# State of the scans: from a running sum in SBUF to identity products in PSUM

## The chip, the cores and the metric

The kernel runs on 1 core of one Trainium2 chip. The metric is device time in microseconds of one execution; three runs of the kernel before gave 2300.24 to 2307.2 us, median 2306.48. Names of engines in the profile: PE is the tensor engine's matmul, PEld its weight load, DVE the vector engine, ACT the scalar engine, POOL GpSimd, SP the queue that issues most transfers.

## The reference, cut to what matters

Two layers are computed for 512 tokens and 256 context tokens of width 1024: an RWKV-7 mixer (layer 0) and a Hyena mixer (layer 1). The change lies in the RWKV-7 scan, which runs once in each direction (z = 0, 1) over context and then over the tokens:

```python
def step(s, inp):
    r_t, w_t, k_t, v_t, a_t, b_t = inp
    sa = jnp.einsum('bhvk,bhk->bhv', s, a_t)
    s = s * w_t[:, :, None, :] + sa[..., None] * b_t[:, :, None, :] + v_t[..., None] * k_t[:, :, None, :]
    return s, jnp.einsum('bhvk,bhk->bhv', s, r_t)
...
for z in range(2):
    yc_z, s_ctx = rwkv7_scan(rc, dc, kdc, vc, kkc, ac, s0, z == 1)
    yx_z, _ = rwkv7_scan(rx, dx, kdx, vx, kkx, ax, s_ctx, z == 1)
```

There are 32 heads of 64 by 64 state; everything is float32.

## The kernel before, in words

The scan is done in chunks of 64 tokens (C): 4 chunks of context and 8 of tokens, so NC = 12 steps of a chain. Heads come in pairs that fill the 128 partitions (p = 0 to 15). One round of the function `chain` takes two pairs (q = 0, 1), two directions (z) and two heads (h) side by side, so a step works on quads of 8 products of 64x64; there are 8 rounds, one after another, 96 steps in all.

A step goes so. The state of head h lies in `sv[h]` on the 64 partitions HR[h]; on the other 64 lie the chunk's values. Eight products of `AR` (keys a, and strictly lower products) with `sv` go to a quad in bank 2 (`bx`, kind pa); ACT copies the half h = 0 to `xs`, DVE the half h = 1. Eight products with the inverse `tt` of a triangular matrix give `bu` (pa again), which ACT and DVE copy, a half each, over the state in `sv`. Then eight products with `BT` (keys b and k, transposed) give `bs` in bank 3 (kind pn, two halves of a bank in turn). DVE adds `bs` to `sc`, a running copy of the state in SBUF, and multiplies it by the chunk's decay `gv`, once for each half, into the next step's `sv`; POOL multiplies `sc` by `gv` as well, in place, for the next step's add. For chunks of tokens (g = 1, 2) eight products `by` of the state with r (ahead of `bu`) and eight more of `sv` with `ARB` (at the step's end) form the output of the step, which the lane `outputs` evacuates.

Round this chain other functions work: `fetch` loads keys, decays and r of a pair and group of four chunks (14 transfers on SP, most of 64 or 128 KB) into rings of GB = 4 and KB = 3 buffers, which the chain gives back when a group of four steps is done; `prep` multiplies them, masks them on DVE and transposes them to `BT` (tile bt, two copies a pair); `merge` loads and completes the inverses; `values` copies values into coming `sv` tiles on ACT or POOL; `readout` and `out_part` turn finished pairs into the layer's output projection (the products whi, wlo with uh, ul). A group's first step begins in program order behind the last copy of its two preparations.

The order on every engine is written ahead of time. Each function is a generator of instructions (a lane); the function `run` picks, by a model of each engine's clock, the instruction that could start first, with a small bias by lane (the chain -0.2 us, preparation 0). Engines then run their own lists in order and wait on semaphores. An instruction made by `copy` with a tuple of engines, or by `either`, is given to the engine on which the model has it done first; the model treats two accesses to one PSUM bank as exclusive. All instructions are emitted in one helper, so that the profile shows line 58 for all of them, and tiles tell them apart: `ps` is any PSUM bank, `cst` the constants (the identity among them).

Of the kernel before, what the change touches and what calls it, by code (L numbers as in the profile page):

```python
# [17 lines left out]
P = 128  # L18
# [7 lines left out]
C = 64  # L26
NCC, NCX = TC // C, TX // C
NC = NCC + NCX
# [211 lines left out]
def net_kernel(ctx: ExitStack, tc: tile.TileContext, I, out, dbg=None):  # L240
    nc = tc.nc
    model = Model()
    V, S, T, G, SP = (Engine(e, n) for e, n in ((nc.vector, "V"), (nc.scalar, "S"), (nc.tensor, "T"), (nc.gpsimd, "G"), (nc.sync, "P")))
    dma = SP.dma_start
    MUL, ADD, SUB = ALU.mult, ALU.add, ALU.subtract
# [81 lines left out]
    def tl(pool, name, shape, bufs=1, dt=F32, tag=None):  # L327
        return model.new(pool, name, shape, bufs, dt, tag)
# [45 lines left out]
    def pt(kind):  # L374
        i = turn[kind]
        turn[kind] = (i + 1) % len(kinds[kind])
        return kinds[kind][i]

    def get(kind):

        return (yield from several(kind, 1))[0]
# [21 lines left out]
    def copy(eng, out, in_):  # L403
        if isinstance(eng, tuple):
            op = copy(eng[0], out, in_)
            op.alts = [op] + [copy(e, out, in_) for e in eng[1:]]
            return op
        if eng is S:
            return S.activation(out=out, in_=in_, func=AF.Copy)
        return eng.tensor_copy(out=out, in_=in_)  # L410
# [14 lines left out]
    def K(name):  # L425
        o, w = CST[name]
        return cst[:, o:o + w]

    ident, ones, cent, ones64 = K("ident"), K("ones"), K("cent"), K("ones64")
# [300 lines left out]
    HR = [slice(0, 64), slice(64, 128)]  # L730
# [261 lines left out]
    n = 2 * sum(g != 3 for g, _, _ in seq)  # L992
# [306 lines left out]
    def rt(name, shape, bufs=1, dt=F32):  # L1299
        return tl(rx, name, shape, bufs, dt)  # L1300
# [14 lines left out]
    xs = rt("xs", [P, 2, 2, 2, C])  # L1315
# [13 lines left out]
    def two(a, b):  # L1329

        return slice(a, b + 1, b - a) if b > a else slice(a, b - 1 if b > 0 else None, b - a)
# [160 lines left out]
    def chain(r):  # L1492

        ps_ = 2 * r, 2 * r + 1
        QZH = [(q, z, h) for q in range(2) for z in range(2) for h in range(2)]

        def quad(kind):
            return pt(kind).rearrange("p (q z t) -> p q z t", q=2, z=2)

        while not all(p in pr for p in ps_):  # L1500
            yield
        gam, _, ptok = rounds[r]
        gf = gam.rearrange("p q c z -> p q (c z)")
        tt = [tts[p % len(tts)] for p in ps_]
        while not svs:
            yield
        sv, stok = svs.pop(0)
        for h in range(2):
            yield G.memset(sv[h][HR[h]], 0.0)
        sc = rt("sc", [P, 2, 2, C])  # L1510
        yield G.memset(sc, 0.0)
        for n in range(NC):
            g, i = divmod(n, 4)
            base, lc = BASE[g], (i, 3 - i)
            while not all((p, g) in grp for p in ps_):
                yield
            AR, ARB, BT, tok = zip(*[grp[p, g] for p in ps_])
            if n == 4:
                while yring.full():
                    yield  # L1520
                yb = tl(rv, "yb", [P, 2, NCX, C], YB), yring.take(), []
            bx = quad("pa")
            for q, z, h in QZH:
                yield T.matmul(bx[HR[h], q, z, :], lhsT=AR[q][z][h][:, 0, lc[z], :], rhs=sv[h][:, q, z, :], start=True, stop=True)

            for h, e in enumerate((S, V)):
                yield copy(e, xs[HR[h], h], bx[HR[h]])
            if g:

                by, ytok = yield from get("py")  # L1530
                by = by.rearrange("p (q z t) -> p q z t", q=2, z=2)
                for q, z, h in QZH:
                    yield T.matmul(by[HR[h], q, z, :], lhsT=sv[h][:, q, z, :], rhs=AR[q][z][h][:, 1, lc[z], :], start=q + z == 0, stop=False)
            while not all(p in mrgd for p in ps_):
                yield
            bu = quad("pa")
            for q, z, h in QZH:
                yield T.matmul(bu[HR[h], q, z, :], lhsT=tt[q][:, z, base[z] + lc[z], :], rhs=xs[:, h, q, z, :], start=True, stop=True)
            for h, e in enumerate((S, V)):
                yield copy(e, sv[h][HR[h]], bu[HR[h]])  # L1540
            if n < NC - 1:
                bs = quad("pn")
                for q, z, h in QZH:
                    yield T.matmul(bs[HR[h], q, z, :], lhsT=BT[q][z][:, lc[z], HR[h]], rhs=sv[h][:, q, z, :], start=True, stop=True)
                yield V.tensor_tensor(out=sc, in0=bs, in1=sc, op=ADD)
                while not svs:
                    yield
                nsv, ntok = svs.pop(0)
                gv = gf[:, :, two(2 * (base[0] + lc[0]), 2 * (base[1] + lc[1]) + 1)].unsqueeze(3).broadcast_to([P, 2, 2, C])
                for h in range(2):  # L1550
                    yield V.tensor_tensor(out=nsv[h][HR[h]], in0=sc[HR[h]], in1=gv[HR[h]], op=MUL)
                if n < NC - 2:
                    yield G.tensor_tensor(out=sc, in0=sc, in1=gv, op=MUL)
            if g:
                for q, z, h in QZH:
                    yield T.matmul(by[HR[h], q, z, :], lhsT=sv[h][:, q, z, :], rhs=ARB[q][:, h, z, lc[z], :], start=False, stop=q + z == 2)
                ys.todo.append((outputs, r, yb, by, ytok, base, lc, n - 4))
            stok[0] = True
            if i == 3:
                for t in tok:  # L1560
                    t[0] = True
            if n < NC - 1:
                sv, stok = nsv, ntok
        ttfree.update(ps_)
        ptok[0] = True
# [110 lines left out]
    def ready_merge(p):  # L1676
# [4 lines left out]
    ends = [reads, parts, Lane([(out_part, p) for p in range(0, NP, 2)], 1, lambda *a: bool(xp), OB)]  # L1681
    rr = range(NP // 2)
    scans = [Lane([(values, r) for r in rr], 1, lambda *a: True, B_VAL), Lane([(chain, r) for r in rr], 1, lambda *a: bool(zeroed), B_CHAIN),
             Lane([(merge, p) for p in range(NP)], 1, ready_merge, B_MERGE), ys, Lane([(fetch, *x) for x in order], 1, lambda *a: bool(zeroed)), Lane([(prep, *x) for x in order], W_PREP, lambda *a: True, B_PREP), invs]
    G2BIAS = 0
# [405 lines left out]
```

## Time and profile before

| | |
|---|---|
| median of 3 runs | 2306.48 us (2300.24 to 2307.2) |
| profiled execution, its own time | 2299.21 us |
| its span, first to last instruction | 2297.5 us |
| mean granted clock of TensorE | 0.94 of full speed |
| busy over the span | PE 88%, PEld 70%, DVE 72%, ACT 46%, POOL 16% |
| moved | 369.39 MB, mean 161 GB/s |

Busy is the share of time in which an engine has an instruction in work; matmuls overlap one another, and their ends are modelled, so that a busy PE is not PE at its peak. A matmul in float32 shows as two records.

### The profile page before, as it was taken

Reading aid. Unit: us, or ns where it says so; the run is one execution under the profiler, and the core shown is the slowest. Engines: PE = TensorE matmul, PEld = TensorE weight load, DVE = VectorE, ACT = ScalarE, POOL = GpSimd, SP = SyncE. Lnnn points to the kernel's source line nnn. Section 1 sums busy time; section 2 is a strip of 40 time slices with the busy share of each in tenths; the row PEclk is TensorE's granted clock in tenths of the full one; section 3 lists DMA queues with packets and bytes.
Section 4 is the critical chain, followed back from the end, with each engine's and each line's share of the span. In section 5 each row is a group of like instructions: output and inputs, shape, how many; then the busy total and the mean of one; then the engine's idle time right before and its main releaser. Section 6 shows DMA issues by size and latency. Waiting matters only on the chain. (4 is left out here: it accounts for less than half of the span.)

```text
span 2297.5 us, 53254 instructions
## 1 busy us (share of the span) xinstructions
PE 2012.7 (88%) x21678; PEld 1600.8 (70%) x21678; DVE 1650.1 (72%) x2624; ACT 1067.1 (46%) x1898; POOL 371.8 (16%) x574
## 2 busy tenths in 40 slices
PE   6699899998976787788988889888599999999997
PEld 2488777776754566676776767766477788878786
DVE  1956378999996869767576666766777576767676
ACT  2444588888762333345353453443453333333333
POOL 0400100000001322323223243221322000000000
PEclk8799999999988887999999999999799999999999
DMA  7055757795787884657566575543664423222232
GB/s 246 34 184 188 233 173 233 247 263 181 212 278 216 207 190 111 172 141 188 137 166 149 144 179 140 145 132 111 197 191 156 147 79 106 82 96 94 87 123 75
DMA packets 317628, 369.39 MB, mean 161 GB/s; under 512 B 132387, under 2 KB 203630, under 8 KB 317384
## 3 DMA queue, kind: packets, MB, share of 16 engines
q1 hardware_dynamic: 303752, 330.21, 49.3%
q0 software_dynamic: 13632, 35.78, 5.3%
q8 instruction: 171, 2.80, 0.5%
q14 instruction: 73, 0.60, 0.1%
HBM read 262.79 MB, written 102.30 MB: 159 GB/s over the span
## 5 line engine op out<-in xcount | busy, mean ns | idle before, releaser
L58 PE MATMUL ps<-m,whi 128*128 128x512 f32 (+1 forms) x1536 | 418.5, 374 | 47.7 <-ACT whi L58 19.0
L58 ACT ACTIVATE whi<-wraw 128x512 fp32r<-128x512 f32 x320 | 200.5, 628 | 385.4 <-PE ps L58 288.9
L58 DVE TENSOR_TENSOR wlo<-wraw,whi 128x512 fp32r<-128x512 f32 x320 | 229.6, 719 | 193.7 <-ACT whi L58 191.2
L58 PEld LDWEIGHTS ps<-m,whi 128*128 128x128 f32 x1536 | 262.4, 196 | 105.9 <-ACT whi L58 20.8
L58 PE MATMUL ps<-m,wlo 128*128 128x512 f32 (+1 forms) x768 | 245.8, 370 | 4.6 <-DVE wlo L58 4.5
L58 PE MATMUL ps<-ar,bk 128*64 128x64 f32 (+2 forms) x4096 | 216.7, 243 | 33.3 <-DVE ar L58 17.8
L58 PEld LDWEIGHTS ps<-ar,bk 128*64 128x64 f32 (+1 forms) x4096 | 184.6, 141 | 55.0 <-issue 24.5
L58 PE MATMUL ps<-h1h,whi 128*128 128x512 f32 x512 | 201.8, 394 | 2.4 <-ACT whi L58 1.4
L58 PE MATMUL ps<-h1h,wlo 128*128 128x512 f32 x512 | 201.2, 393 | 0.7 <-DVE wlo L58 0.7
L58 PE MATMUL ps<-h1l,whi 128*128 128x512 f32 x512 | 201.0, 393 | 0.0
L58 PEld LDWEIGHTS ps<-m,wlo 128*128 128x128 f32 x768 | 133.1, 196 | 31.1 <-DVE wlo L58 6.7
L58 DVE TENSOR_TENSOR ar<-ps,cst 64x512 f32<-64x512 f32 (+1 forms) x192 | 114.8, 599 | 22.9 <-PE ps L58 17.9
L58 POOL TENSOR_TENSOR sc<-sc,gam 128x256 f32<-128x256 f32 x80 | 56.4, 705 | 428.0 <-DVE sv L58 420.2
L58 PEld LDWEIGHTS ps<-h1h,whi 128*128 128x128 f32 x512 | 96.7, 189 | 22.1 <-ACT whi L58 1.8
L58 PEld LDWEIGHTS ps<-h1h,wlo 128*128 128x128 f32 x512 | 97.0, 189 | 21.1 <-DVE wlo L58 1.2
L58 PEld LDWEIGHTS ps<-h1l,whi 128*128 128x128 f32 x512 | 96.8, 189 | 20.0 <-DVE h1l L58 0.5
L58 PE MATMUL ps<-sv,bt 128*64 128x64 f32 x1408 | 89.1, 236 | 16.8 <-DVE sv L58 9.5
L58 DVE TENSOR_TENSOR ltm<-lt 128x90 f32<-128x90 f32 (+14 forms) x120 | 81.4, 678 | 29.2 <-DMA wraw<-wg 17.6
L58 ACT ACT_TABLE_LOAD x76 | 97.5, 1283 | 8.1 <-DMA aw<-ada_w 5.9
L58 PEld LDWEIGHTS ps<-sv,bt 128*64 128x64 f32 x1408 | 66.9, 142 | 41.8 <-DVE sv L58 15.8
L58 ACT ACTIVATE sv<-ps 64x256 f32<-64x256 f32 x96 | 36.1, 376 | 125.9 <-PE ps L58 122.2
L58 PE MATMUL ps<-xs,tt 128*64 128x64 f32 x1536 | 68.6, 232 | 28.2 <-DVE xs L58 26.0
(289 smaller groups left out, 4426.4 us busy)
## 6 DMA issues: line engine op xcount, KB each, us to landing
wraw<-wg SPq DMA_DIRECT2D x128, 256.0 KB
wraw<-w SPq DMA_DIRECT2D x128, 256.0 KB
aw<-ada_w SPq DMA_DIRECT2D x96, 256.0 KB
bkd<-bk SPq DMA_DIRECT2D x32, 768.0 KB
ard<-ar SPq DMA_DIRECT2D x32, 640.0 KB
ar<-ard SPq DMA_DIRECT2D x128, 128.0 KB
ar<-zd SPq DMA_DIRECT2D x128, 128.0 KB
wraw<-w_out SPq DMA_DIRECT2D x64, 256.0 KB
```

The lines of the kernel that those rows point to most:

```text
L58: return getattr(self.eng.eng, self.fn)(*self.a, **self.k)
```

## The change

The running copy `sc` in SBUF goes, with its memsets, DVE's add and POOL's product. In its place, in every step but a round's last, eight products with the identity as weights copy the state from `sv` into the quad `bs` in bank 3, behind the copies to `xs` in the chain's order and ahead of `by`; the products with `BT` then accumulate on them in the same PSUM group, and the products with `gv` read `bs` from PSUM. Beside that the four copies of a step (to `xs`, to `sv`) are offered to ACT and DVE, whichever the planner has done first, in place of one half for each.

```diff
--- before.py
+++ after.py
@@ -1507,8 +1507,6 @@
         sv, stok = svs.pop(0)
         for h in range(2):
             yield G.memset(sv[h][HR[h]], 0.0)
-        sc = rt("sc", [P, 2, 2, C])
-        yield G.memset(sc, 0.0)
         for n in range(NC):
             g, i = divmod(n, 4)
             base, lc = BASE[g], (i, 3 - i)
@@ -1523,10 +1521,14 @@
             for q, z, h in QZH:
                 yield T.matmul(bx[HR[h], q, z, :], lhsT=AR[q][z][h][:, 0, lc[z], :], rhs=sv[h][:, q, z, :], start=True, stop=True)
 
-            for h, e in enumerate((S, V)):
-                yield copy(e, xs[HR[h], h], bx[HR[h]])
+            for h in range(2):
+                yield copy((S, V), xs[HR[h], h], bx[HR[h]])
+
+            if n < NC - 1:
+                bs = quad("pn")
+                for q, z, h in QZH:
+                    yield T.matmul(bs[HR[h], q, z, :], lhsT=ident[:, HR[h]], rhs=sv[h][:, q, z, :], start=q + z == 0, stop=False)
             if g:
-
                 by, ytok = yield from get("py")
                 by = by.rearrange("p (q z t) -> p q z t", q=2, z=2)
                 for q, z, h in QZH:
@@ -1536,21 +1538,17 @@
             bu = quad("pa")
             for q, z, h in QZH:
                 yield T.matmul(bu[HR[h], q, z, :], lhsT=tt[q][:, z, base[z] + lc[z], :], rhs=xs[:, h, q, z, :], start=True, stop=True)
-            for h, e in enumerate((S, V)):
-                yield copy(e, sv[h][HR[h]], bu[HR[h]])
+            for h in range(2):
+                yield copy((S, V), sv[h][HR[h]], bu[HR[h]])
             if n < NC - 1:
-                bs = quad("pn")
                 for q, z, h in QZH:
-                    yield T.matmul(bs[HR[h], q, z, :], lhsT=BT[q][z][:, lc[z], HR[h]], rhs=sv[h][:, q, z, :], start=True, stop=True)
-                yield V.tensor_tensor(out=sc, in0=bs, in1=sc, op=ADD)
+                    yield T.matmul(bs[HR[h], q, z, :], lhsT=BT[q][z][:, lc[z], HR[h]], rhs=sv[h][:, q, z, :], start=False, stop=q + z == 2)
                 while not svs:
                     yield
                 nsv, ntok = svs.pop(0)
                 gv = gf[:, :, two(2 * (base[0] + lc[0]), 2 * (base[1] + lc[1]) + 1)].unsqueeze(3).broadcast_to([P, 2, 2, C])
                 for h in range(2):
-                    yield V.tensor_tensor(out=nsv[h][HR[h]], in0=sc[HR[h]], in1=gv[HR[h]], op=MUL)
-                if n < NC - 2:
-                    yield G.tensor_tensor(out=sc, in0=sc, in1=gv, op=MUL)
+                    yield V.tensor_tensor(out=nsv[h][HR[h]], in0=bs[HR[h]], in1=gv[HR[h]], op=MUL)
             if g:
                 for q, z, h in QZH:
                     yield T.matmul(by[HR[h], q, z, :], lhsT=sv[h][:, q, z, :], rhs=ARB[q][:, h, z, lc[z], :], start=False, stop=q + z == 2)
```

## Rows read from the trace of the kernel before

**Rows 1.** Page, busy us (share of the span) x instructions.

```profile
PE 2012.7 (88%) x21678; PEld 1600.8 (70%) x21678; DVE 1650.1 (72%) x2624; ACT 1067.1 (46%) x1898; POOL 371.8 (16%) x574
```

**Rows 2.** Instructions by tile sv: duration ns min/median/max, first and last start us.

```profile
L58 PE MATMUL ps<-sv,ar x1536: 219/222/371, 835.2 to 1594.3; 128*64 128x64 f32 x192
```

**Rows 3.** Busy us (x instructions) by engine from 835 to 1598 us; clock, DMA, GB/s.

```profile
835.00:1598.00 763.00, 657.52 (x13595) 530.86 (x13596) 535.77 (x1011) 320.01 (x649) 230.31 (x382) 0.94 0.59 147
```

**Rows 4.** Timeline of one step, 1588 to 1594 us: start, us, engine, operation, [idle before].

```profile
1588.26 0.64 PE L58 MATMUL ps<-sv,ar 128*64 128x64 f32 x16
...
1588.82 0.68 DVE L58 TENSOR_TENSOR x<-ps,x 128x512 f32<-128x512 f32 x1
...
1588.94 0.38 ACT L58 ACTIVATE xs<-ps 64x256 f32<-64x256 f32 x1 [3.45 <-PE ps L58]
...
1588.96 0.69 PE L58 MATMUL ps<-ar,sv 128*64 128x64 f32 x16
...
1589.53 0.43 DVE L58 COPY xs<-ps 64x256 f32<-64x256 f32 x1
...
1590.02 0.69 PE L58 MATMUL ps<-xs,tt 128*64 128x64 f32 x16 [0.37 <-DVE xs L58]
...
1590.63 0.50 PE L58 MATMUL ps<-whi,uh 128*128 128x512 f32 x1
...
1590.74 0.38 ACT L58 ACTIVATE sv<-ps 64x256 f32<-64x256 f32 x1 [1.43 <-PE ps L58]
...
1591.53 0.79 PE L58 MATMUL ps<-sv,bt 128*64 128x64 f32 x16
...
1592.42 0.42 DVE L58 TENSOR_TENSOR sc<-ps,sc 128x256 f32<-128x256 f32 x1 [0.84 <-PE ps L58]
...
1592.88 0.87 DVE L58 TENSOR_TENSOR sv<-sc,gam 64x256 f32<-64x256 f32 x2
...
1593.66 0.54 PE L58 MATMUL ps<-sv,ar 128*64 128x64 f32 x5
```

**Rows 5.** Timeline, SP, PE, DVE and ACT, at a group's start (1133 to 1204 us).

```profile
1133.35 0.69 PE L58 MATMUL ps<-sv,ar 128*64 128x64 f32 x16
...
1157.38 1.74 SPq L58 DMA_DIRECT2D bk<-bkd  x2
1163.53 0.39 SPq L58 DMA_DIRECT2D aw<-ada_w  x1
...
1189.55 0.60 SPq L58 DMA_DIRECT2D ar<-zd  x1
...
1203.22 0.64 PE L58 MATMUL ps<-sv,ar 128*64 128x64 f32 x16
1203.25 0.59 ACT L58 ACTIVATE bt<-ps 128x512 f32<-128x512 f32 x1
```

**Rows 6.** Waits from 835 to 1598 us: who for whom, us, times, longest.

```profile
SPq L58 <- PE ps L58: 112.4, 70, 11.0
...
DVE xs L58 <- ACT xs L58: 30.9, 40, 2.7
...
PE ps L58 <- DVE xs L58: 26.0, 29, 7.1
...
PE ps L58 <- DVE sv L58: 16.0, 33, 2.2
```

**Rows 7.** Groups of operations, 835 to 1598 us: count | busy, mean ns | idle before.

```profile
L58 DVE TENSOR_TENSOR sv<-sc,gam 64x256 f32<-64x256 f32 x176 | 80.2, 456 | 5.5
...
L58 POOL TENSOR_TENSOR sc<-sc,gam 128x256 f32<-128x256 f32 x80 | 56.4, 705 | 428.0 <-DVE sv L58 420.2 <-PE ps L58 7.7
...
L58 DVE COPY xs<-ps 64x256 f32<-64x256 f32 x96 | 41.0, 427 | 33.0 <-ACT xs L58 30.9
...
L58 DVE TENSOR_TENSOR sc<-ps,sc 128x256 f32<-128x256 f32 x88 | 37.2, 422 | 41.6 <-PE ps L58 39.1
```

**Rows 8.** Instructions by tile sc, 835 to 1598 us, columns as in rows 2.

```profile
L58 DVE TENSOR_TENSOR sv<-sc,gam x176: 416/421/3484, 855.4 to 1593.3; 64x256 f32<-64x256 f32 x176
```

## The prediction, made blind

> **What bounds the kernel now.** Read first the page's busy shares: PE stands at 88% of the span [rows 1], so no stage leaves the tensor engine much room, and the question is what bounds the one stage that the change touches. The scans' products run from 835.2 to 1594.3 us [rows 2]; 95 steps lie between those starts, some 7.99 us each. Over 835 to 1598 us PE is busy 657.5 of 763 us (86%), DVE 535.8 (70%), ACT 320.0 (42%), POOL 230.3 (30%) [rows 3]. No engine is full; PE is the nearest, with 763 - 657.5 = 105.5 us idle.
>
> Next a single step in the timeline, where the reader sees the chain [rows 4]. From 1588.26 (the AR products, state by transformed keys) it goes: ACT copies half of xs, DVE the other half, 16 PE records (xs times tt) at 1590.02, ACT and DVE copies into sv, the keys' products at 1591.53, DVE's add into sc at 1592.42, two DVE products to 1593.75, and the next step's first product at 1593.66. That is 5.40 us, one operation behind the other. The mean of 7.99 therefore holds some 2.6 us a step that this chain alone doesn't need.
>
> Where that goes is seen at a group's start (a group is four steps) [rows 5]. SP stands from 1159.12 to 1163.53 until the chain's group that began at 1133.35 is done, then issues the loads of the group after the next until 1190.15; the preparation ends with a copy into bt from 1203.25, and the chain's first product of that group starts at 1203.22. So two group periods, 1133.35 to 1203.22 = 69.9 us, are made of one group of four chain steps (1133.35 to SP's restart at 1163.53), one round of loads (to 1190.15) and one preparation (to 1203.8). SP's wait for PE is the longest of its waits in the stage, 112.4 us in 70 times [rows 6]. The stage is a loop: chain, loads, preparation, with two groups in flight. I therefore count what is taken off the chain at half.
>
> **The change part by part.**
>
> *The add goes.* Each of 8 rounds has 11 steps with one, so 88 adds of 0.42 us [rows 7]. In the step shown it holds the chain from 1592.42 to 1592.88, 0.46 us with its hand-over. 88 x 0.46 = 40.5 us off the chain. What is late next is the wait of the same DVE queue for the keys' products, which is unchanged, and then the two products with gamma.
>
> *POOL's products and memsets on sc go*: 80 of 0.705 us, 56.4 us [rows 7]. POOL idles 428.0 us ahead of them, waiting for DVE; they end long before the next add needs them. Off the path: nothing, and no cover is lost.
>
> *The products with gamma read PSUM.* 176 of 0.42 us by the median [rows 8]. No such row exists before; the nearest are the add (one PSUM operand, 128x256, 0.42) and the copies from PSUM (0.427) [rows 7]. So the price is between 0 and 176 x 0.006 = +1.1 us. The other way: their mean of 0.456 gives 80.2 us, 6.1 more than 176 x 0.421, and one took 3.48 us [rows 7, 8]; with the POOL product gone, and one operand from PSUM, some of that excess should go. I take -3 (between -6.1 and +1.1).
>
> The Trainium skill, "SBUF — State Buffer", section "Who interferes with whom", says that a vector instruction with two SBUF inputs contends with a GpSimd instruction that reads SBUF and that the later one blocks until the first is done. The 3.48 us row agrees with that; no run yet shows the form with one SBUF input. By the rule the whole 6.1 us would go, which moves the sum by 3.
>
> *Copies by choice.* Four a step (two of xs, two of sv) were fixed, half of them on DVE. The halves of one tile don't run side by side: DVE waited 30.9 us for ACT's xs half [rows 6], and in the step shown the DVE copy at 1589.53 came after a 0.68 us accumulation, while ACT had idled 3.45 us before its half and 1.43 after [rows 4]. Two halves on ACT in a row cost 0.38 + 0.38, against 0.38 + 0.43, so order costs nothing, and a late DVE is avoided. PE waited 26.0 us in 29 times for DVE's xs half [rows 6]. At best all 26.0 go. At worst the choice sends halves to DVE that ACT had: 192 x 0.05 = +9.6 us. I take half of the best, -13, since ACT has its own queue (42% busy) and the choice is made ahead of time, by planned and not by real clocks.
>
> So the chain is shorter by 40.5 + 3 + 13 = 56.5 us, and by the half rule the stage by 28.
>
> *The identity products come.* 88 x 8 products, each of two records: 88 x 16. Sixteen records of the same shape (64 columns, 128x64 weights) issue in 0.64 less the last one's 0.22 = 0.42 us (1588.26), up to 0.69 - 0.22 = 0.47 [rows 2, 4]. With 0.46: 88 x 0.46 = 40.5 us of PE work, by coincidence what the adds took from DVE. They stand behind the state's products and ahead of by, where PE waits for the xs copies: from 1588.68 to 1590.02 in the step shown, 1.34 us, of which by needs 0.47. 0.47 + 0.46 = 0.93, so the chain itself is not held. What is queued behind them on PE: by, and the preparation and output products that used to fill that gap (at 1590.63 such output products fill the next one). These move into other gaps. Nothing is charged if the 105.5 us idle takes them; 40.5 if it takes none. I charge them where a group is held by its preparation, 13.7 of 35 us (1190.15 to 1203.8, of a period of 69.9 / 2), 39%: 0.39 x 40.5 = 16, counted at half as one preparation stands in two periods: +8. The wait that they add is for a free half of a PSUM bank whose last reader is the product with gamma of the step before, already waited for by the state's products: nothing.
>
> The Trainium skill, "Perfetto Trace Analysis", section "Identifying the Most-Contended Engine", says that matmul busy time is a poor measure of the tensor engine's room and that weight-load busy time is a better one. That is 530.9 of 763 us, 70% [rows 3]; by it the products would fit for nothing and the sum would be 8 us lower. I stay with the matmul rows, since the weight loads of 64 columns run beside them.
>
> *DVE is lighter* by 37.2 us of adds and by the halves that leave it, which helps the mask products of the preparation: by the same share and half, 0.39 x 37.2 / 2 = 7 at best, 0 if PE ends last there. I take -2.
>
> **Sum.** -28 + 8 - 2 = -22 us. The profiled execution took 2299.2 us (span 2297.5): 2277. The median of the runs is 2306.5, 7.3 above the profiled one, so the forecast for the median is 2306.5 - 22 = 2284. A change of less than 0.3% (7 us) can't be told from none.
>
> **The rivals.**
>
> *PE becomes the bound (slower).* PE's 105.5 us idle must fall below 65 for the identity products to cost nothing. The waits named for the xs half make 26.0 of it and those for DVE's sv 16.0 [rows 6]; if the shorter chain only closes half of the former (13) and the displaced products find no gap, the stage grows by 40.5 - 13 = 27 us: 2334. It decides from the point where PE is over 91% busy ((657.5 + 40.5) / 763) in a stage of the old length. For it: 86% now, and gaps mid-step are already filled with output products [rows 4]. Against it: ahead of group starts the chain waits, and PE with it. Chance 0.25; 2314 to 2346.
>
> *The groups don't move (no change).* The loads take 1163.53 to 1190.15 of the period, on SP's own pace, with one transfer behind the other; if loads and preparation take up all that the chain gives back, a step ends earlier and the group's start waits longer. For it: SP issues are nearly unbroken there. Against: SP waited for the chain to begin. Time 2306, within 7. Chance 0.17.
>
> *All of the chain counts.* If preparation keeps up once DVE and POOL are lighter, 56.5 us go and the products hide: 2250, from 2240 to 2268. For it: the floor of 5.40 against 7.99. Against: the loop above. Chance 0.12.
>
> *The choice does nothing*: if each half lands where it was, term four is 0, the chain gives 43.5, half of it 22, and the sum is -16: 2290, inside the forecast's own range.
>
> **How the numbers follow.** The forecast has 0.46, with its own range 2268 to 2299. Faster by over 0.3%: 0.46 + 0.12, less 0.01 for the upper edge of its own range: 0.57. Same: 0.17 + 0.01 = 0.18. Slower: 0.25. The range of 2244 to 2326 leaves out some 0.05 below and 0.13 above.
>
> **What would show it.** Right: steps inside a group shorter by 0.4 to 0.6 us, the DVE add gone and its place between the keys' products and the products with gamma empty; PE's busy time in the stage about 698 us with idle under 65; the starts of the scans still set by copies into bt; more than half of the xs and sv halves on ACT. Wrong: steps as long as before with PE busy over 93% (PE bound), or steps shorter and the waits ahead of group starts longer by the same amount (no move), or a stage under 715 us (all counts). The stages outside 835 to 1598 us should keep their lengths; if they don't, something is moved that I have not seen.

## The result, and the profile after

The changed kernel takes 2278.35 us (median of 4 runs, 2274.53 to 2280.25) against 2306.84 for the kernel before on the same chip: a ratio of 0.9884 [0.9863, 0.9905], 28.5 us faster. The forecast was 2284. The profiled execution has a span of 2272.8 us against 2297.5.

Page of the kernel after, answering to [rows 1]: busy us (share of the span) x instructions.

```profile
span 2272.8 us, 55896 instructions
...
PE 2018.4 (89%) x23086; PEld 1625.6 (72%) x23086; DVE 1555.1 (68%) x2428; ACT 1102.4 (49%) x1992; POOL 316.2 (14%) x500
```

PE executed 1408 more records in a span 24.7 us shorter, DVE is 95 us lighter, ACT 35 heavier. Where the time went is seen in the stage of the scans, then in the stage behind it. The columns are the stretch, its length, busy us (x instructions) of PE, PEld, DVE, ACT and POOL, the granted clock of TensorE, the DMA share and GB/s.

```profile
833.00:1570.00 737.00, 656.45 (x14956) 549.45 (x14955) 438.32 (x802) 351.82 (x737) 175.72 (x309) 0.96 0.61 151
1570.00:2272.00 702.00, 645.03 (x2991) 525.81 (x2989) 486.49 (x776) 261.50 (x435) 57.08 (x55) 0.97 0.39 123
```

The same for the stretch behind the stage in the kernel before (its stage is in [rows 3]):

```profile
1598.00:2297.00 699.00, 635.44 (x2946) 517.89 (x2944) 483.49 (x762) 257.71 (x430) 57.89 (x55) 0.96 0.38 122
```

The stage went from 763 to 737 us, and what follows it grew by 3 (702 against 699, with 45 more PE records). Two things in these rows matter later. PE's busy time in the stage did not rise by the products added: 656.5 against 657.5. And the granted clock rose from 0.94 to 0.96: as the level is either full or half, 2 x 0.04 x 737, about 59 us, at half clock here, against 2 x 0.06 x 763 = 92 before (54.6 and 95.6 us when the clock's own records are added up).

Tile sv of the kernel after, answering to [rows 2, 8]: duration ns min/median/max, first and last start, forms.

```profile
L58 PE MATMUL ps<-sv,ar x1536: 219/222/369, 833.6 to 1565.8; 128*64 128x64 f32 x192
...
L58 PE MATMUL ps<-sv,cst x1408: 217/222/369, 834.8 to 1561.5; 128*64 128x64 f32 x176
...
L58 DVE TENSOR_TENSOR sv<-ps,gam x176: 378/423/429, 851.4 to 1564.8; 64x256 f32<-64x256 f32 x176
L58 ACT ACTIVATE sv<-ps x175: 377/379/380, 849.9 to 1568.4; 64x256 f32<-64x256 f32 x175
...
L58 DVE COPY sv<-ps x17: 408/418/428, 956.7 to 1527.0; 64x256 f32<-64x256 f32 x17
```

Tile xs, the same columns:

```profile
L58 ACT ACTIVATE xs<-ps x147: 364/379/382, 834.4 to 1566.5; 64x256 f32<-64x256 f32 x147
...
L58 DVE COPY xs<-ps x45: 416/427/430, 903.2 to 1554.3; 64x256 f32<-64x256 f32 x45
```

`ps<-sv,cst` are the identity products. ACT now has 322 of the 384 halves of xs and sv (half before). The products with gamma have lost their long ones: at most 429 ns, where one took 3484 [rows 8].

One step in the timeline of the kernel after (start us, us, operation, records, [idle before]), answering to [rows 4]:

```profile
1559.59 0.64 PE L58 MATMUL ps<-sv,ar 128*64 128x64 f32 x16
...
1560.61 0.78 ACT L58 ACTIVATE xs<-ps 64x256 f32<-64x256 f32 x2 [2.86 <-PE ps L58]
...
1561.05 0.69 PE L58 MATMUL ps<-sv,cst 128*64 128x64 f32 x16
...
1561.57 0.64 PE L58 MATMUL ps<-ar,sv 128*64 128x64 f32 x16
...
1562.03 0.64 PE L58 MATMUL ps<-xs,tt 128*64 128x64 f32 x16
...
1562.72 0.78 ACT L58 ACTIVATE sv<-ps 64x256 f32<-64x256 f32 x2 [1.32 <-PE ps L58]
...
1563.15 1.08 PE L58 MATMUL ps<-sv,bt 128*64 128x64 f32 x16
...
1564.34 0.88 DVE L58 TENSOR_TENSOR sv<-ps,gam 64x256 f32<-64x256 f32 x2 [0.51 <-PE ps L58]
...
1565.34 0.67 PE L58 MATMUL ps<-sv,ar 128*64 128x64 f32 x16
```

The add is gone: DVE waits 0.51 us for the keys' products and goes on with gamma. But xs is ready at 1560.61 + 0.78 = 1561.39, and the products that read it start at 1562.03, 0.64 us later: the identity products and `by` (`ps<-ar,sv`) stand ahead of them on PE. Before, PE had idled 0.37 us for the DVE copy and started 0.06 us behind its end (1589.53 + 0.43, then 1590.02) [rows 4].

Two group periods of the kernel after, answering to [rows 5]:

```profile
1124.77 0.69 PE L58 MATMUL ps<-sv,ar 128*64 128x64 f32 x16
...
1148.00 1.25 SPq L58 DMA_DIRECT2D bk<-bkd  x2
...
1177.99 0.61 SPq L58 DMA_DIRECT2D ar<-zd  x1
...
1192.53 0.60 ACT L58 ACTIVATE bt<-ps 128x512 f32<-128x512 f32 x1 [0.77 <-PE ps L58]
...
1193.18 0.69 PE L58 MATMUL ps<-sv,ar 128*64 128x64 f32 x16
```

As before, the group's first product follows the last copy into bt (1193.13, then 1193.18). Two periods are 68.4 us against 69.9.

Two more rows of the kernel before belong beside [rows 5]. They show what ends ahead of SP's issue at 1163.53, and when the group that began at 1133.35 gives way to the next:

```profile
1163.05 0.42 PE L58 MATMUL ps<-aw,cpad 128*32 128x128 f32 x8
...
1168.53 0.70 PE L58 MATMUL ps<-sv,ar 128*64 128x64 f32 x8
```

To see this for all 96 steps I split the time from the first step's start to the last one's into four sums. Chain: from a step's first AR product to the end of its second product with gamma (88 steps). Group waits: from there to the next step's start where a new group begins (16 places). Other: the same gap at the other steps; it can be negative. Round ends: the last steps of seven rounds. In us:

| kernel | chain (mean) | group waits | other | round ends | in all |
|---|---|---|---|---|---|
| before | 609.5 (6.93) | 79.8 | 15.4 | 53.8 | 758.5 |
| after | 564.1 (6.41) | 98.3 | 2.5 | 66.8 | 731.7 |

Chain and other fell by 58.3, for which the prediction had 56.5. Group waits and round ends grew by 31.5, or 54% of it, for which it had "half". What is left is 26.8 us.

### The profile page after: what moved, and what is told of

It is laid out like the page before. It is cut to its first block, busy times and chain, and to the rows that moved or that the text cites. A ratio compares the mean times of both kernels' runs of the same rounds, so it can differ in the third digit from the quotient of the medians.

```text
span 2272.8 us, 55896 instructions
## 1 busy us (share of the span) xinstructions
PE 2018.4 (89%) x23086; PEld 1625.6 (72%) x23086; DVE 1555.1 (68%) x2428; ACT 1102.4 (49%) x1992; POOL 316.2 (14%) x500
## 4 chain that ended last, share of the span: by engine, by line
PE 58%; DVE 14%; DMA 9%; ACT 5%; issue 4%; SPq 3%; POOL 1%; DVEq 0%; ACTq 0%; POOLq 0%
PE ps L58 58%; SPq L58 3%; DMA ar<-zd 2%; DVE wlo L58 2%; DVE bk L58 2%; DVE lt L58 2%; DVE ltm L58 1%; DVE ar L58 1%; DMA ar<-ard 1%; DMA wraw<-wg 1%; DVE cvv L58 1%; ACT sv L58 1%; DMA tt<-td 1%; DVE ta L58 1%; DMA lt<-ld 1%
## 5 line engine op out<-in xcount | busy, mean ns | idle before, releaser
L58 DVE TENSOR_TENSOR wlo<-wraw,whi 128x512 fp32r<-128x512 f32 x320 | 224.7, 703 | 183.7 <-ACT whi L58 173.8
L58 PE MATMUL ps<-ar,bk 128*64 128x64 f32 (+2 forms) x4096 | 210.1, 241 | 45.8 <-DVE ar L58 16.6
L58 DVE TENSOR_TENSOR sv<-ps,gam 64x256 f32<-64x256 f32 x176 | 74.2, 422 | 76.3 <-PE ps L58 63.0
L58 ACT ACTIVATE sv<-ps 64x256 f32<-64x256 f32 x175 | 66.2, 378 | 119.9 <-PE ps L58 113.3
L58 POOL COPY sv<-vt 64x256 f32<-64x256 f32 x99 | 41.3, 417 | 499.0 <-PE ps L58 392.3
L58 PE MATMUL ps<-sv,ar 128*64 128x64 f32 x1536 | 80.2, 232 | 19.3 <-DVE sv L58 18.0
```

The costliest lines, as they stand in the source:

```text
L58: return getattr(self.eng.eng, self.fn)(*self.a, **self.k)
```

## The experiments

Theories ahead of the runs: (A) the shorter chain counts at about half, the loop of chain, loads and preparation taking back the rest, and the identity products cost little; (B) it is the copies by choice that pay. A third (C) came up with the first results: the written order, which is drawn anew for each kernel, moves the time by itself. Ratios are to the kernel before in the same runs, with 95% intervals.

**Choice alone.** The kernel before, with its four copies a step offered to both engines.

```diff
-            for h, e in enumerate((S, V)):
-                yield copy(e, xs[HR[h], h], bx[HR[h]])
+            for h in range(2):
+                yield copy((S, V), xs[HR[h], h], bx[HR[h]])
```

(and the same for `sv` and `bu`)

> The kernel before with the four copies of a step on ACT or DVE by choice, and nothing else (the add, sc and POOL's product stay). Loop theory (chain, loads, preparation, two groups in flight; what the chain gives back counts half): the forecast's term of 13 us off the chain, so 6 to 7 us faster, and up to 20 if the xs and sv ends move as far as they did with the whole change (0.39 and 0.26 us a step, 96 steps, at half 31). Rival that PE sets the end: no PE work goes, 0 (within 5 us). Rival that the choice alone carries the whole gain: 25 to 31 us faster.

2277.86 us, 0.9876 [0.9843, 0.9909]: as much as the whole change. Its stage:

```profile
839.00:1588.00 749.00, 651.29 (x13605) 528.44 (x13604) 484.12 (x894) 375.13 (x789) 221.84 (x360) 0.94 0.61 150
```

The stage is only 14 us shorter (749 against 763); what follows it is 9 shorter and what leads up to it 4 longer. That makes the 20 us by which the two profiled executions differ (2277.3 against 2297.5); the profiled one of the kernel before lies 8 us under its median. In the stage chain and other fell by 14.9 us, and the waits took nothing back.

**Identity alone.** The kernel after with the copies fixed again, half on ACT and half on DVE.

> The changed kernel with the four copies bound as before (first half ACT, second half DVE). Loop theory: the add's 40.5 us and 3 of the products with gamma at half, less 8 for the identity products, plus 2 for a lighter DVE: 16 us faster than before, so 2291. Rival that PE sets the end: 704 products cost 40.5 us less what idle time takes; 0 to 27 us slower than before. Rival that the identity part carries the whole gain: 25 to 31 us faster.

2296.48 us, 0.9957 [0.9936, 0.9978]. The two parts alone make -29.2 and -10.6, together -28.5: they don't add. Here chain and other fell by 52.2 and the waits grew by 54.4, so the stage kept its length, with the identity products inside it:

```profile
834.00:1600.00 766.00, 678.57 (x14965) 564.37 (x14964) 480.13 (x913) 309.13 (x629) 175.95 (x308) 0.94 0.60 145
```

**Identity products twice.** A second set with a weight of zeros on the same state, into the same group.

```diff
                 for q, z, h in QZH:
                     yield T.matmul(bs[...], lhsT=ident[:, HR[h]], rhs=sv[h][:, q, z, :], start=q + z == 0, stop=False)
+                for q, z, h in QZH:
+                    yield T.matmul(bs[...], lhsT=nought, rhs=sv[h][:, q, z, :], start=False, stop=False)
```

> The changed kernel with eight more products of the same shape in every step but a round's last, with zeros as weights, into the same PSUM group behind the identity products: 704 products, 40.5 us of PE work more, nothing else. Loop theory as forecast: 8 us slower than the changed kernel; with the hold of the products xs times tt that its trace shows (they start 0.82 us behind the copies, where it was 0.20), all 40.5 on the chain at half: up to 20 slower, 2286 to 2299. PE sets the end: 40 slower, 2318. PE's idle time takes them: 2278.

2307.62 us, 1.0013 [0.9995, 1.0032]: 29.3 us above the kernel after. Its stage, and then both sets of products in it (busy us, mean ns | idle before):

```profile
833.00:1606.00 773.00, 697.90 (x16376) 590.70 (x16376) 443.21 (x808) 349.01 (x733) 180.13 (x318) 0.97 0.59 144
```

```profile
L58 PE MATMUL ps<-sv,cst 128*64 128x64 f32 x1408 | 64.0, 233 | 0.0
...
L58 PE MATMUL ps<-sv,nought 128*64 128x64 f32 x1408 | 60.2, 226 | 1.0 <-issue 1.0
```

PE's busy time rose by 41.5 us over the kernel after (697.9 against 656.5) at nearly the same clock, the stage by 36. The start of the xs products falls further behind: 1.28 us behind the copies in the mean of the steps, where after has 0.84 and before 0.32. Chain and other are 28.9 us longer than in the kernel after. So most of the work isn't taken by gaps; it holds the chain.

**No identity products.** The kernel after without them, the keys' products starting the group; so it leaves out the state before the chunk.

```diff
-                for q, z, h in QZH:
-                    yield T.matmul(bs[...], lhsT=ident[:, HR[h]], rhs=sv[h][:, q, z, :], start=q + z == 0, stop=False)
...
-                    yield T.matmul(bs[...], lhsT=BT[...], rhs=sv[h][:, q, z, :], start=False, stop=q + z == 2)
+                    yield T.matmul(bs[...], lhsT=BT[...], rhs=sv[h][:, q, z, :], start=q + z == 0, stop=q + z == 2)
```

> The changed kernel without the identity products: the state before the chunk is left out of the next state, so its values are not the scan's; the instructions, their order rules and the rest of the work are the same. Loop theory: 8 to 20 us faster than the changed kernel, 2258 to 2270. PE sets the end: 40 us faster, 2238. Products free: 2278.

2255.61 us, 0.9781 [0.9743, 0.9819]: 22.7 below the kernel after. The chain is shorter, with the xs products 0.47 us behind the copies. In the timeline of a step (xs ready at 1560.33, products at 1560.38):

```profile
1559.55 0.78 ACT L58 ACTIVATE xs<-ps 64x256 f32<-64x256 f32 x2
...
1560.38 0.69 PE L58 MATMUL ps<-xs,tt 128*64 128x64 f32 x16 [0.23 <-ACT xs L58]
```

But the stage itself is no shorter than that of the kernel after:

```profile
832.00:1573.00 741.00, 649.32 (x13580) 531.07 (x13579) 443.92 (x813) 351.37 (x741) 175.66 (x304) 0.92 0.62 151
```

1376 records fewer, and PE's busy time falls by only 7 us: the clock is 0.92, some 2 x 0.08 x 741 = 119 us at half level. The stage is 4 us longer than in the kernel after (740.2 against 735.9, from first AR product to last ARB product); what follows it is 15.8 us shorter (687.5 against 703.3). The profiled executions are 12.6 us apart (2260.2 against 2272.8), and none of it lies in the stage: the gain is not read where the products stood.

**Identity in wide products.** Two products of 256 columns, in place of eight of 64.

```diff
-                for q, z, h in QZH:
-                    yield T.matmul(bs[...], lhsT=ident[:, HR[h]], rhs=sv[h][:, q, z, :], start=q + z == 0, stop=False)
+                for h in range(2):
+                    yield T.matmul(bs[HR[h]], lhsT=ident[:, HR[h]], rhs=sv[h], start=True, stop=False)
```

> The changed kernel with the eight identity products of 64 columns made two of 256 columns (same weights for four quads): the same columns stream, a quarter of the weight loads and instructions. Theory that the identity products cost 23 to 29 us (the runs with none and with twice as many) because their columns take PE's time and hold the products xs times tt: 0 to 5 us faster than the changed kernel. Rival that their count of instructions and weight loads is the price: 12 to 20 faster, 2258 to 2266.

2302.02 us, 0.999 [0.9971, 1.001], 24 above the kernel after. A quarter of the instructions has the same busy time, 63.1 us against 63.6 in the kernel after (busy us, mean ns | idle before):

```profile
L58 PE MATMUL ps<-sv,cst 128*64 128x256 f32 x352 | 63.1, 416 | 0.0
```

Chain and other fell by 76.8 us against before, 18.5 more than in the kernel after, and the waits took back 78.6. So fewer instructions and weight loads save no PE time, and a shorter chain alone is no gain.

**Zero loads from POOL.** In the kernel after, the 8 of 28 loads of a group that fill `AR` with zeros are issued by POOL, to see whether SP's own pace sets the loads.

```diff
-                yield dma(out=AR[z][h][HR[1 - h], 0:na]..., in_=zd[:, 0:na])
+                yield G.dma_start(out=AR[z][h][HR[1 - h], 0:na]..., in_=zd[:, 0:na])
```

> The changed kernel with the zero halves of the keys (8 of 28 transfers of a group) issued by POOL in place of SP. Loop theory (loads on SP's own pace, 27 of two periods): 8 x 0.6 = 4.8 us less a round of loads, half of it a period, 22 groups: up to 53 us faster, at least 15. Theory that PE's time, not the loop, sets the end: 0, within 7 us of 2278.

2286.71 us, 0.9919 [0.9894, 0.9944], 8 us above the kernel after. A round of loads from its first ard issue to the end of its last ard or zero issue (mean of 21 groups) is 23.3 us, against 23.7 in the kernel after. SP waits more, for PE (us, times, longest; first the kernel after, then this run):

```profile
SPq L58 <- PE ps L58: 115.2, 60, 10.4
...
SPq L58 <- PE ps L58: 188.1, 70, 17.5
```

So SP was not short of time: its loads wait for buffers that PE's work frees. Most of these are not the scans' loads. Of the 188.1 us, 24 are waits of key loads (`ar<-ard`) and 76 those of `aw<-ada_w`, weights of another function, which stand in the same queue ahead of keys (28 and 18 in the kernel after).

**Choice for xs alone, and all four copies on ACT.** Both on the kernel before.

```diff
+            for h in range(2):
+                yield copy((S, V), xs[HR[h], h], bx[HR[h]])
```

(the first; the second has `copy(S, ...)` for xs and for sv)

> The kernel before with the choice for the two copies to xs alone. Theory that the gain comes where PE waited for DVE's half of xs (26.0 us in the stage before): most of the choice's 29 us, 18 to 29 faster than before. Rival that the halves of sv matter as much: 10 to 16 faster. Rival that a changed order of the whole list, not the copies, made the gain: any value, 0 as well.

> The kernel before with all four copies of a step on ACT, no choice. If the gain is that copies leave a late DVE (with the choice ACT took 338 of 384): 20 to 32 us faster than before, as the choice. Rival that the choice itself is needed, since ACT is late in turn behind its table loads of 1.28 us: 5 to 15 faster.

2306.77 us, 0.9995 [0.997, 1.0019], and 2303.83 us, 0.9995 [0.9978, 1.0012]. Neither gains. In the first, PE's waits in the stage (us, times, longest) show that what I had counted on did happen:

```profile
PE ps L58 <- DVE sv L58: 37.4, 45, 9.5
...
PE ps L58 <- DVE xs L58: 4.9, 4, 1.7
```

The wait for DVE's xs half fell from 26.0 to 4.9 us, and that for DVE's sv rose from 16.0 to 37.4 [rows 6]. With all on ACT, chain and other fell by 18.6 us, more than in the choice alone, and the waits grew by 27.4. The mechanism of the copies is there both times; the gain of the choice alone isn't explained by it.

**Other orders of the same work.** To test (C), both kernels with the planner's bias of the chain at -0.15 and at -0.25, which changes the order on the engines (and, through it, some engine choices), not the work.

```diff
-    B_CHAIN = -0.2
+    B_CHAIN = -0.15
```

> The kernel before with the planner's bias of the chain at -0.15 us in place of -0.2: the same instructions of the scans in another order. Theory that the scan stage's time follows from the work: 2305, within 7. Rival that it follows from the list as drawn (order alone moves it as the seven variants so far suggest): 8 to 25 us off, either way.

> The changed kernel with the same bias, -0.15. Work theory: 28 us faster than the kernel before with that bias, within 9. Order theory: the distance between the two at equal bias differs from 28 by more than 12 us, and may have the other sign.

> The kernel before with the bias of the chain at -0.25. Work theory: 2305, within 7. Order theory: 8 to 25 us off, either way.

> The changed kernel with the bias at -0.25. Work theory: 28 us faster than the kernel before with that bias, within 9. Order theory: the distance differs from 28 by more than 12 us, and may have the other sign.

| bias | before | after | difference |
|---|---|---|---|
| -0.15 | 2338.38, 1.0147 [1.0106, 1.0188] | 2324.86, 1.008 [1.0054, 1.0106] | -13.5 |
| -0.20 | 2306.84, 1 | 2278.35, 0.9884 [0.9863, 0.9905] | -28.5 |
| -0.25 | 2286.25, 0.9916 [0.9886, 0.9946] | 2291.41, 0.9947 [0.9924, 0.997] | +5.2 |

The order alone moves the kernel before by +32 and -20 us, and the kernel after by +46 and +13. At -0.25 the change loses clear of noise: all nine runs of the kernel after (2289.91 to 2298.82) lie above all five of the kernel before (2282.34 to 2288.64). The stage in the kernel before at -0.15:

```profile
834.00:1657.00 823.00, 676.22 (x13605) 555.92 (x13604) 533.91 (x1013) 328.16 (x661) 225.84 (x368) 0.88 0.55 137
```

The kernel before at -0.25:

```profile
836.00:1592.00 756.00, 658.11 (x13586) 532.15 (x13584) 532.64 (x1009) 319.69 (x650) 230.51 (x378) 0.94 0.59 148
```

The kernel after at -0.25:

```profile
836.00:1594.00 758.00, 679.24 (x14991) 567.71 (x14991) 448.52 (x819) 355.47 (x748) 169.97 (x292) 0.95 0.59 148
```

The four sums, for these pairs and the others (us, change against the kernel before, at equal bias where a bias is named):

| kernel | chain and other | group waits and round ends | taken back |
|---|---|---|---|
| after, -0.20 | -58.3 | +31.5 | 54% |
| after, -0.15 | -51.2 | +28.7 | 56% |
| after, -0.25 | -49.2 | +53.3 | 108% |
| identity alone | -52.2 | +54.4 | 104% |
| wide identity products | -76.8 | +78.6 | 102% |
| zero loads from POOL | -66.7 | +63.4 | 95% |
| identity products twice | -29.4 | +38.5 | 131% |
| choice alone | -14.9 | -0.1 | 0% |

## Why the prediction was right, and where it was not

At the order as drawn, the sign, the size and the place were right: 2278 for 2284, with the gain in the stage of the scans. By its steps:

- *The add goes.* Right: from the last keys' product's start to gamma, the mean fell from 0.94 to 0.55 us, 34 us over 88 steps for 40.5 forecast.
- *The chain's sum.* The chain of a step fell from 6.93 to 6.41 us, within the 0.4 to 0.6 announced (at -0.15 and -0.25 only by 0.19 and 0.27, the rest in the gap to the next step), and chain and other by 49 to 58 us at three biases, against 56.5. But the terms are not those of the forecast. The xs copies end 33 us earlier over the 88 steps, and the products that read them start 46 us later behind these copies, a hold that the forecast had at nothing; the rest of the step (sv copies, the products with gamma, the gap to the next step) gives the other 37. That the sum fits is in part luck.
- *The products with gamma read PSUM* (-3, between -6.1 and +1.1). The saving was at the lower end: 74.2 us for 176 of 0.422 against 80.2, so 6.0. The Trainium skill, "SBUF — State Buffer", section "Who interferes with whom", has a vector instruction contend with GpSimd when both its inputs are in SBUF. The trace agrees: before, nine of these products began while POOL had a copy, a mask or a `bo` product in work, and eight of the nine took 567 to 3484 ns; after, 27 began so, and none took over 427. The product with sc was beside none of the long ones, so that its going is not the reason. By the half rule the whole 6.1 would have moved the sum by 1.5 us, not by the 3 that the prediction says.
- *Copies by choice* (-13 on the chain, half of it -6.5). The step that failed is "at best all 26.0 go" read as time won. In the choice for xs alone the wait did go, and the next one (DVE's sv) grew by 21.4 us. The choice alone measured -29, but xs alone and all on ACT measured nothing, so that -29 can't be put down to the copies either.
- *The identity products come* (+8). Mis-sized, through the sentence "0.47 + 0.46 = 0.93, so the chain itself is not held". The gap of 1.34 us was read from one step in which the second xs half came late on DVE. Once that lateness is off (copies' end 1.56 us behind the last AR product's start before, 1.18 after), the gap is shorter than what stands in it, and PE holds the chain: 0.84 us from copies to xs products against 0.32 before and 0.47 with the set left out. A second set costs 29.3 us of its 40.5. Leaving the set out gives 22.7, but not in the stage, where its work was. So 23 to 29 us, three times the forecast, is what these two runs give, each with an order of its own; as orders move the time by as much, the hold on the chain is shown, the price is not. The Trainium skill, "Perfetto Trace Analysis", section "Identifying the Most-Contended Engine", judges the tensor engine's headroom by weight-load time and not by matmul time; by it the prediction's aside had the products fit for nothing. The second set left room by that measure, with weight loads at 76% (590.7 of 773 us), and the kernel took 29 us longer; what work costs that stands in a chain's way is not read from it.
- *PE's busy time of 698 us with idle under 65*: wrong, 656 and 80. Two things hide the 40.5 us of products. Half-clock time fell by 41 us, and PE was busy in 44 us of it against 78; as the records of xs times tt stand 53 ns apart at half clock and 31 at full (means in the kernel before), that is some 14 us of PE time, as an estimate. And output products (whi, wlo with uh, ul) moved: 36 sets of them are left behind the stage's end, against 16, and 20 sets of three at 0.23 us are 14. That also is why *the stages outside keep their lengths* failed: from the stage's end to layer 1's first product went from 76.5 to 85.8 us. The rest, some 13 us, I can't place.
- *The half rule.* 54% was taken back, as forecast, yet as a rule it isn't shown. The other lists give from 0 to 131%, mostly about all. The loop's closing step held (by the median of its groups a kernel starts one within some 0.3 us of the last copy into bt). Its opening step was misread: at 1163.53 SP did not wait for the chain's group, whose four steps last until the next group starts at 1168.53, but for the last product that reads `aw`, as the two rows above show; the load that then starts is `aw<-ada_w` [rows 5]. Of SP's 112.4 us of waits for PE only 33.0 are those of key loads (`ar<-ard`). "On SP's own pace" fell too: with 8 of 28 issues taken off SP, the round of loads is as long. The rival *the groups don't move*, which rested on that pace, names the outcome of most variants and of the pair at -0.25, with another cause. What holds the next group stays open; preparation ends last, PE's work is in it and in the buffers that it needs, but no run tried them apart.
- *PE becomes the bound*: did not come, at 656.5 of 737 us (89%). The doubled products, at 90%, are where it nearly did: busy and stage then grow together (+41 and +36).

What the prediction lacked altogether is the draw. Edited, the kernel gets a new order on all engines, and order alone moved the time from -20 to +46 us. Of the 28.5 us, only about 12 (the mean of -13.5, -28.5 and +5.2) is what the change does over three orders, and three differences this far apart leave its sign unsure. So the forecast's closeness is largely luck: the chain's sum came out by other terms, and the list gave back no more than half of it.

Open: which property of a list does it. Less idle on PE and less half-clock time go together (idle in the stage 80 us and half clock 55 after, 106 and 96 before, 147 and 191 in the kernel before at -0.15), but which is the cause was not tried apart, nor was an order held fixed under the change. Where the choice alone wins its 29 us stays open with it.

## What to carry to other kernels

Where a planner writes the order of all engines, measure an edit at several of its settings before you credit it: one setting here says -28.5 us, another +5. Work that "fills a gap" ahead of a chain's wait must be weighed against the gap that is left when the wait is cured by the same change. What a shorter chain is worth is read from the waits ahead of the next group, not from the chain.

## What the runs showed of the hardware

- Eight identity products of 64 columns (16 records) and two of 256 columns (4 records) have nearly the same busy time over the stage, 63.6 us (1408 records of 232 ns, overlapping) and 63.1 us (352 of 416 ns), and hold PE until the next product starts for 0.52 and 0.48 us (medians): fewer, wider instructions saved PE next to nothing.
- Two ACT copies of half a tile in a row took 0.78 us together, against 0.38 and 0.43 on two engines [rows 4]; where the halves don't overlap, as here, the split gains nothing.
- The mean granted clock of the same work in the stage went from 0.88 to 0.94 by the order alone (the kernel before at -0.15, and at -0.20 and -0.25).
- A DVE product of two SBUF tiles that begins while POOL computes is held (eight of nine, up to 3484 ns for 421); with one of the two in PSUM it is not (27 of 27 at most 427 ns).
